# Moving half of an output projection in among attention units, in a one-core streaming-encoder layer

## The chip, the cores and the metric

The kernel runs on one core of a Trainium2 chip. The time is device microseconds of that core for one launch; the profile is one execution of its own, recorded by the hardware profiler. TensorE does the matmuls and transposes, ScalarE, VectorE and GpSimd the rest, and nearly all transfers are issued from SyncE's queue (SP).

## What is computed

One layer for 1024 prompt tokens and 32 sample tokens (1056 rows of 1024). Cut to what matters here:

```python
proj = x @ w_in
o_a = latent attention, 8 heads of 64            # "A", 512 columns of mix
o_b = rms(differential attention, 4 heads of 128)  # "B", 512 columns of mix
mix = concatenate([o_a, o_b], -1)
h = LN1(ALPHA * x + mix @ w_o)
h = LN2(ALPHA * h + ConvGLU(h))
y = h + sigmoid(h @ w_ple_gate + b) * (p @ w_ple_proj)
```

All of it is in 32-bit precision. A matmul of the projections runs as three matmuls on a split of each operand into a high and a low part (`three`, lines 144 to 146); for the sample rows as two (`sample_rows`, lines 152 and 153). Splitting (`split`) is a ScalarE copy of the high part (line 85) and a VectorE subtraction of it (line 82).

## The kernel before, in words

The program is traced in Python and then planned: each engine gets a static list in an order that a planner makes from the order in the text and from its own costs, and tiles take slots of small pools: 22 `pair`s (`HP`, tag h) for most operands, 4 `slab`s, 2 `stg`, 2 `srow`, and in PSUM 4 banks `pm` and 2 double banks `pd`. `paced` and `held` put an instruction in the plan not ahead of the last marked one; they add no wait on the chip.

- Attention is 32 units of `UnitB` (4 heads, 8 row blocks from the last to the first) and then 64 of `UnitA` (8 heads). `front` makes a block's scores (lines 554 and 555 for B, `three` into `pd` for A), the softmax's maximum on VectorE (line 524) and the exponential on ScalarE. `back` comes two or three units later; it transposes the probabilities (lines 575 and 804), copies them out of PSUM (line 576; a `split` in A) and multiplies with the values (lines 579 and 813). `hook(n, ...)` puts other work ahead of unit n: preparation of keys and queries (`prep_a`, `unpark`, with copies in SBUF through SP at lines 731 and 756), and the sample rows' latent attention at 84 to 95.
- The results are `mixB` (B, features by tokens) and `mixA` (A).
- The output projection comes after attention, for the sample tile 8 and then tiles 7 to 0: once with `w_o` columns 0 to 255 for all nine, once with 256 to 511, each with all eight blocks of 128 features, B's first (the two passes of the loop over `i`), and then with columns 512 to 1023 inside `h_rows`. `mix_in` splits a tile's four feature pairs; `residual` (line 1026) adds ALPHA times x, which `x_back` has loaded.
- `h_rows` goes on with the first norm (`unit`), `h_turn` transposes the normed row and applies gain and bias (line 1087 on TensorE, line 1090 on VectorE and 1092 on ScalarE in turns), and `h_pair` and `h_sample` make the sums of blocks (`combos`) with which the up-projection does seven block products instead of eight. `UpWeights.part` makes the weights' sums; the first pair's seven parts run in the second pass of the projection.
- The up-projection (lines 1205 to 1207), from 731 us on, the down-projection and the gate follow; the change does not touch them.

Of the kernel before, what the change touches and what calls it, by code (L numbers as in the profile page):

```python
# [16 lines left out]
DEC = 32  # L17
# [20 lines left out]
def layer(ctx: ExitStack, tc: tile.TileContext, a, o):  # L38
# [497 lines left out]
    class UnitB:  # L536
# [26 lines left out]

        def back(self):
            h, i, p2 = self.h, self.i, self.p
            ss = UnitB.group[h, i // 4]
            if i % 4 == 3:
                UnitB.po = pm((128, 4, 128))
            po = UnitB.po
            pT = slab((128, 8, 128))  # L570
            for k0 in range(0, i + 1, 4):
                kn = min(4, i + 1 - k0)
                pt = pm((128, 4, 128))
                for j in range(kn):
                    PE.transpose(pt[:, j], p2[:, 0, (k0 + j) * 128 : (k0 + j + 1) * 128], ident)
                ACT.copy(pT[:, k0 : k0 + kn], pt[:, :kn])
            ii = i % 4
            for k in range(i + 1):
                PE.matmul(po[:, ii], pT[:, k], dv[k // 4][:, k % 4, h * 128 : (h + 1) * 128], start=(k == 0), stop=(k == i))  # L579
            ACT.activation(pT[:, 0], po[:, ii], AF.Square, accum_out=ss[:, 4 + ii : 5 + ii])  # L580
            if ii:
                return

            DVE.scalar_tensor_tensor(ss[:, 8:12], ss[:, 0:4], EPS, ss[:, 0:4], ALU.mult, ALU.mult)
            DVE.scalar_tensor_tensor(ss[:, 8:12], ss[:, 4:8], 1.0 / 128.0, ss[:, 8:12], ALU.mult, ALU.add)
            POOL.tensor_tensor(ss[:, 12:16], ss[:, 8:12], neghalf[:, 0:1].to_broadcast([128, 4]), ALU.pow)
            ob = srow() if h == 3 else small(512, tag="sam", bufs=1)
            for q in range(4):
                DVE.scalar_tensor_tensor(ob[:, q * 128 : (q + 1) * 128], po[:, q], ss[:, 12 + q : 13 + q], g8, ALU.mult, ALU.mult)
            hook(UnitB.step + 3, lambda: self.finish(ob))  # L590
# [176 lines left out]
    class UnitA:  # L767
# [20 lines left out]

        def back(self):
            h, i, p = self.h, self.i, self.p  # L790
            vt = L["vt"][h // 4]
            j, ib = divmod(i, 2)
            kt = 2 * (j + 1)
            if ib:
                UnitA.pts = [pair((128, 2, 4, 256)) for _ in range((kt + 3) // 4)]
            pts = UnitA.pts
            if i in (7, 3):
                UnitA.po = pm()
            po = UnitA.po
            for k0 in range(0, i + 1, 4):  # L800
                kn = min(4, i + 1 - k0)
                pt = pm((128, 4, 128))
                for jj in range(kn):
                    PE.transpose(pt[:, jj], p[:, (k0 + jj) * 128 : (k0 + jj + 1) * 128], ident)  # L804
                d = pts[k0 // 4]
                UnitA.turned = split(d[:, 0, :kn, 128 * ib : 128 * ib + 128], d[:, 1, :kn, 128 * ib : 128 * ib + 128], pt[:, :kn])
            if ib:
                POOL.memset(f(pts[-1][:, :, (kt - 1) % 4, 0:128]), 0.0)
                return
            c = 256 * (j % 2)  # L810
            for k in range(kt):
                for hl in range(2):
                    PE.matmul(po[:, c : c + 256], vt[k // 4][:, k % 4, h % 4], pts[k // 4][:, hl, k % 4],  # L813
                              start=(k == 0 and hl == 0), stop=(k == kt - 1 and hl == 1))
            if j % 2 == 0:
                e = h % 2
                own, oth = slice(64 * e, 64 * e + 64), slice(64 - 64 * e, 128 - 64 * e)
                d = hd(L["mixA"], h // 2)[own, 256 * j : 256 * j + 512]
                ACT.copy(d, po[oth])
                DVE.tensor_tensor(d, po[own], d, ALU.add)  # L820
# [101 lines left out]
                ACT.copy(L["mixA"][g][64 * e : 64 * e + 64, :, S0:T], v[64 * e : 64 * e + 64, 2 * g : 2 * g + 2, e])  # L922

    w_o = a["w_o"].rearrange("(k p) c -> p k c", p=128)
    wb = []

    def wo_block(c, N):
        per = 1024 // N
        return [wload([(0, 1024, w_o[:, (4 + i * per) % 8 : (4 + i * per) % 8 + per, c : c + N])], 1024) for i in range(8 // per)]


    units = [UnitB(h, i) for h in range(4) for i in range(7, -1, -1)]
# [32 lines left out]
    for n, s in enumerate((sa_load, sa_query, lambda: sa_keys(0), lambda: sa_keys(1), sa_rotary, lambda: sa_scores(0),  # L965
                           lambda: sa_scores(1), lambda: sa_turn(0), lambda: sa_turn(1), lambda: sa_values(0), lambda: sa_values(1), sa_end)):
        hook(84 + n, s)
    hook(94, lambda: gate.__setitem__(0, UnitA.last), lambda: wb.append(wo_block(0, 256)))

    waiting = []  # L970
    for n in range(len(units)):
        UnitB.step = n
        for s in hooks.setdefault(n, []):
            s()
        units[n].front()
        waiting.append(units[n])
        while len(waiting) > (2 if n < 8 or n >= 32 else 3):
            waiting.pop(0).back()
    for n, u in enumerate(waiting):
        for s in hooks.get(len(units) + n, ()):  # L980
            s()
        u.back()
    mixA = L["mixA"]
    gate[0], mark[0] = UnitA.last, UnitA.turned


    acc = [pair((128, 2, 1024), F32) for _ in range(4)]
    acc_s = cpool.tile([DEC, 1024], F32, name="acc_s", tag="x4")
    order = (8, 7, 6, 5, 4, 3, 2, 1, 0)

# [2 lines left out]


    mixp = {}
    msam = small(512, F32R, tag="sam", bufs=1).rearrange("p (k h c) -> p k h c", k=8, h=2)

    def mix_in(t):

        c0, n = TOK[t]  # L1000
        d = mixp[t] = pair((128, 8, 2, 128)) if t < 8 else msam
        for i in range(4):
            src = (mixB if i < 2 else mixA)[i % 2][:, :, c0 : c0 + n]
            split(d[:, 2 * i : 2 * i + 2, 0, :n], d[:, 2 * i : 2 * i + 2, 1, :n], src, pace=t < 7)

    mix_in(8)

    def proj_rows(t, wk, N):

        n = TOK[t][1]  # L1010
        ps = pm()
        d = mixp[t]
        if t < 8:
            three(ps[:, :N], [(d[:, k, 0], d[:, k, 1], *wk(k)) for k in range(8)])
            return ps[:, :N], None
        sample_rows(ps, lambda k: d[:, k].rearrange("p h c -> p (h c)"), wk, 8, N)
        return ps[:DEC, :N], ps[DEC : 2 * DEC, :N]

    def wo_at(ws, N):
        per = 1024 // N  # L1020
        return lambda k: tuple(ws[k // per][:, hl, (k % per) * N : (k % per + 1) * N] for hl in (0, 1))

    def residual(t, c, N, ps, ps2):
        n = TOK[t][1]
        d = arow(t)[:n, c : c + N]
        mark[0] = DVE.scalar_tensor_tensor(d, d, ALPHA, ps, ALU.mult, ALU.add)
        if ps2 is not None:
            lo = small(512, tag="srow", bufs=2)
            ACT.copy(lo[:n, :N], ps2)
            DVE.tensor_tensor(d, d, lo[:n, :N], ALU.add)  # L1030

    def unit(r, n):

# [11 lines left out]
        (eng or POOL).tensor_tensor(r, r, g[:n, :D], ALU.mult)  # L1045
        (eng or POOL).tensor_tensor(r, r, b[:n, :D], ALU.add)

    def x_back(t):
        load(arow(t)[: TOK[t][1]], a["x_p"][t * 128 : (t + 1) * 128, :] if t < 8 else a["x_s"])

    for t in order[:3]:
        x_back(t)
    for t in order[1:3]:
        mix_in(t)

# [24 lines left out]
    def h_turn(t, d):  # L1082

        n = TOK[t][1]
        ps = pd((128, 8, 128))
        for j in range(8):
            PE.transpose(ps[:, j, :n], arow(t)[:n, j * 128 : (j + 1) * 128], ident[:n, :n])
        for j in range(8):
            if j % 2:
                DVE.tensor_scalar(d[:, j], ps[:, j, :n], lnT[:, j : j + 1], lnT[:, 8 + j : 9 + j], ALU.mult, ALU.add)  # L1090
            else:
                ACT.activation(d[:, j], ps[:, j, :n], AF.Identity, bias=lnT[:, 8 + j : 9 + j], scale=lnT[:, j : j + 1])
# [153 lines left out]
    zd = [DR.tile([128, len(fs), T], F32, name=nm("zd")) for fs in GROUPS]  # L1246


    for i in range(2):
        for m, t in enumerate(order):  # L1250
            if i == 0:
                if m == 1:
                    wb.append(wo_block(256, 256))
                if 2 < m + 2 < 9:
                    x_back(order[m + 2])
                    if m:
                        mix_in(order[m + 2])
            elif m == 0:
                wb.append(wo_block(512, 512))
                wts = UpWeights(up_load(0))  # L1260
            if i == 1 and m < NP:
                wts.part(m)
            ps, ps2 = proj_rows(t, wo_at(wb[i], 256), 256)
            residual(t, 256 * i, 256, ps, ps2)


    hrow = [DR.tile([128, 1024], F32, name=nm("hrow")) for _ in range(8)]

    def h_rows(t):
        ps, ps2 = proj_rows(t, wo_at(wb[2], 512), 512)  # L1270
        residual(t, 512, 512, ps, ps2)
        unit(arow(t)[: TOK[t][1]], TOK[t][1])
        if t < 8:
            SP.dma_start(hrow[t], arow(t))


    for t in order[:4]:
        h_rows(t)
    hs = small(512, tag="sam", bufs=1)
    V["hs"], V["hs2"] = hs[:, :256].rearrange("p (k c) -> p k c", k=8), hs[:, 256:512]  # L1280
    h_turn(8, V["hs"])
# [330 lines left out]
```

## Time and profile before

| | |
|---|---|
| median of 3 runs | 1582.12 us (1577.77 to 1582.86) |
| the profiled execution's own time | 1580.15 us |
| its span in the profile | 1578.1 us, mean granted clock 0.986 |
| TensorE busy | 1506.7 us (95%) |
| VectorE, ScalarE, GpSimd busy | 970.7, 716.5, 336.8 us |
| differential units | about 252 to 352 us |
| latent units and their preparation | about 352 to 594 us |
| projection, first norm, block sums | about 594 to 731 us |

All stretches are microseconds from the start of the span. A matmul's busy time holds its way through the array, and consecutive matmuls overlap, so a stretch in which TensorE is shown busy need not be full. Rows of waits name the waiting engine and line, then what released it. "clock" is the granted share of TensorE's full speed.

### The profile page before, as it was taken

Reading aid. Unit: us, or ns where it says so; the run is one execution under the profiler, and the core shown is the slowest. Engines: PE = TensorE matmul, PEld = TensorE weight load, DVE = VectorE, ACT = ScalarE, POOL = GpSimd, SP = SyncE. Lnnn points to the kernel's source line nnn. Section 1 sums busy time; section 2 is a strip of 40 time slices with the busy share of each in tenths; the row PEclk is TensorE's granted clock in tenths of the full one; section 3 lists DMA queues with packets and bytes.
Section 4 is the critical chain, followed back from the end, with each engine's and each line's share of the span. In section 5 each row is a group of like instructions: output and inputs, shape, how many; then the busy total and the mean of one; then the engine's idle time right before and its main releaser. Section 6 shows DMA issues by size and latency. Waiting matters only on the chain.

```text
span 1578.1 us, 25308 instructions
## 1 busy us (share of the span) xinstructions
PE 1506.7 (95%) x9787; PEld 1363.0 (86%) x9787; DVE 970.7 (62%) x1944; ACT 716.5 (45%) x1754; POOL 336.8 (21%) x394
## 2 busy tenths in 40 slices
PE   7999998888989999989999999999989999999998
PEld 7999987777878889878999999999977787876887
DVE  4113336885767757598577777777778524279332
ACT  4223337776777765056455555555543312022111
POOL 0002134632454320010011111111110000049311
PEclk9999999989999999999999999999999999999999
DMA  7113251221110116122222222222265423231111
GB/s 218 38 46 89 81 159 46 43 63 28 25 49 15 51 54 208 41 87 62 80 82 82 82 82 82 82 74 68 91 194 171 146 59 115 80 99 42 41 44 44
DMA packets 125868, 127.89 MB, mean 81 GB/s; under 512 B 14701, under 2 KB 105461, under 8 KB 125493
## 3 DMA queue, kind: packets, MB, share of 16 engines
q1 hardware_dynamic: 125749, 126.28, 26.3%
q8 instruction: 77, 1.26, 0.3%
q14 instruction: 42, 0.34, 0.1%
HBM read 93.83 MB, written 26.07 MB: 76 GB/s over the span
## 4 chain that ended last, share of the span: by engine, by line
PE 81%; DVE 10%; ACT 5%; DMA 2%; issue 2%; POOL 0%; SPq 0%; DVEq 0%; ACTq 0%
PE pm L144 13%; PE pm L146 13%; PE pm L145 13%; PE pd L1207 5%; PE pd L1206 5%; PE pd L1205 5%; PE pm L1205 4%; PE pm L1207 4%; PE pm L1206 4%; DVE h L82 3%; PE pm L813 2%; ACT h L85 2%; PE pm L579 1%; PE pm L804 1%; DVE h L562 1%
## 5 line engine op out<-in xcount | busy, mean ns | idle before, releaser
L144 PE MATMUL pm<-h,h 128*128 128x512 f32 (+4 forms) x1076 | 367.6, 342 | 6.3 <-DVE h L82 3.6
L146 PE MATMUL pm<-h,h 128*128 128x512 f32 (+4 forms) x1076 | 364.4, 339 | 3.6 <-DVE h L82 3.6
L145 PE MATMUL pm<-h,h 128*128 128x512 f32 (+4 forms) x1076 | 363.8, 338 | 0.0
L144 PEld LDWEIGHTS pm<-h,h 128*128 128x128 f32 x1076 | 204.7, 190 | 28.4 <-issue 3.2
L146 PEld LDWEIGHTS pm<-h,h 128*128 128x128 f32 x1076 | 203.5, 189 | 23.7 <-DVE h L82 4.2
L145 PEld LDWEIGHTS pm<-h,h 128*128 128x128 f32 x1076 | 203.8, 189 | 19.5 <-issue 0.5
L85 ACT CAST h<-t 128x1024 fp32r<-128x1024 f32 (+6 forms) x91 | 81.9, 912 | 216.5 <-PE pm L146 102.0
L82 DVE TENSOR_TENSOR h<-t,h 128x1024 fp32r<-128x1024 f32 (+6 forms) x81 | 89.5, 1114 | 96.5 <-ACT h L85 96.3
L82 DVE TENSOR_TENSOR h<-pm,h 128x256 fp32r<-128x256 f32 (+7 forms) x221 | 101.6, 485 | 55.8 <-ACT h L85 53.9
L1218 DVE SCALAR_TENSOR_TENSOR h<-h,cp,h 128x1058 f32<-128x1058 f32 x88 | 115.8, 1316 | 25.4 <-ACT h L1226 24.7
L85 ACT CAST h<-pm 128x256 fp32r<-128x256 f32 (+7 forms) x221 | 88.5, 426 | 53.7 <-PE pm L804 22.1
L1192 ACT COPY h<-pd 128x256 f32<-128x256 f32 (+1 forms) x258 | 56.1, 270 | 115.9 <-PE pd L1207 115.8
L1205 PE MATMUL pm<-h,s 128*128 128x264 f32 x360 | 102.7, 288 | 1.2 <-ACT h L1192 0.9
L1206 PE MATMUL pm<-h,s 128*128 128x264 f32 x360 | 102.0, 286 | 0.4 <-DVE h L82 0.4
L82 DVE TENSOR_TENSOR h<-h,h 128x512 fp32r<-128x512 f32 (+4 forms) x166 | 100.7, 638 | 2.2 <-ACT h L85 2.1
L1207 PE MATMUL pm<-h,s 128*128 128x264 f32 x360 | 99.9, 286 | 0.0
L1205 PE MATMUL pd<-h,s 128*128 128x264 f32 x344 | 97.9, 285 | 0.4 <-DVE h L1090 0.4
L1206 PE MATMUL pd<-h,s 128*128 128x264 f32 x344 | 97.8, 284 | 0.5 <-DVE h L82 0.5
L1207 PE MATMUL pd<-h,s 128*128 128x264 f32 x344 | 98.1, 285 | 0.0
L1367 DVE TENSOR_TENSOR h<-pm,h 128x512 f32<-128x512 f32 x48 | 32.8, 684 | 76.4 <-PE pm L146 76.3
L178 POOL TENSOR_TENSOR sm<-sm,neghalf 128x1 f32<-128x1 f32 (+1 forms) x37 | 23.9, 645 | 253.6 <-DVE sm L177 239.1
L82 DVE TENSOR_TENSOR s<-h,s 128x512 fp32r<-128x512 f32 (+1 forms) x96 | 60.4, 639 | 28.5 <-ACT s L85 28.2
(326 smaller groups left out, 3734.2 us busy)
## 6 DMA issues: line engine op xcount, KB each, us to landing
h<-in_w_up SPq DMA_DIRECT2D x44, 512.0 KB, 4.7
zd<-h SPq DMA_DIRECT2D x22, 529.0 KB, 4.4
t<-zd SPq DMA_DIRECT2D x24, 384.0 KB, 3.6
t<-in_w_down SPq DMA_DIRECT2D x16, 512.0 KB, 3.2
h<-in_x_p SPq DMA_DIRECT2D x15, 512.0 KB, 7.2
t<-in_w_in SPq DMA_DIRECT2D x14, 512.0 KB, 3.8
h<-h SPq DMA_DIRECT2D x8, 512.0 KB, 4.9
t<-in_w_o SPq DMA_DIRECT2D x8, 512.0 KB, 3.4
```

Of the source, the lines that this page charges most:

```text
L82: return eng.tensor_tensor(out, x, y, ALU.subtract)
L85: c = ACT.copy(hi, src)
L144: PE.matmul(ps, sh, mh, start=(i == 0), stop=False)
L145: PE.matmul(ps, sh, ml, start=False, stop=False)
L146: PE.matmul(ps, sl, mh, start=False, stop=(i == last))
L813: PE.matmul(po[:, c : c + 256], vt[k // 4][:, k % 4, h % 4], pts[k // 4][:, hl, k % 4], start=(k == 0 and hl == 0), stop=(k == kt - 1 and ...
L1192: ACT.copy(x, y)
L1205: PE.matmul(ps[:, :BW], w[:, 0, k], c[:, k, 0], start=first and k == 0, stop=False, skip_group_check=True)
L1206: PE.matmul(ps[:, :BW], w[:, 0, k], c[:, k, 1], start=False, stop=False, skip_group_check=True)
L1207: PE.matmul(ps[:, :BW], w[:, 1, k], c[:, k, 0], start=False, stop=k == 3, skip_group_check=True)
L1218: DVE.scalar_tensor_tensor(z[:, j], U[:, j, i : i + T], cp[:, i, m + j * NF : m + j * NF + 1], z[:, j], ALU.mult, ALU.add)
L1367: DVE.tensor_tensor(d, ps[:n], d, ALU.add)
```

## The change

The projection is split by feature half. The B half (blocks 4 to 7 of `w_o`) is done in 36 pieces, four blocks of 256 columns times nine token tiles, hooked ahead of units 38 to 46, 47 to 55, 66 to 74 and 75 to 83, one to a unit. A block loads and splits its weights (`share_w`); a mix tile pair is split once, in the first block, written to DRAM (`hb`) and loaded again in the other three (`share_in`, one unit ahead). A piece (`share`) loads 256 columns of x into an `srow`, does four blocks of three matmuls (for the sample tile two) into a `pm` bank, adds ALPHA times x on VectorE and stores the sum to DRAM (`xw`). The A half is one pass after attention, in `h_rows`: two times 512 columns with four blocks, on rows loaded from `xw`, with the norm right behind. The values of a unit, in A and B, are done one unit after its transposes (`values`). In `h_turn` ScalarE takes columns 0 to 3 and VectorE 4 to 7. The seven parts of the first up-weights run two behind each of the first four `h_rows`.

```diff
@@ class UnitB, UnitA
         def back(self):
...
+        def values(self):
+            h, i, pT = self.h, self.i, self.pT
+            ss = UnitB.group[h, i // 4]
+            if i % 4 == 3:
+                UnitB.po = pm((128, 4, 128))
...
+        def values(self):
+            h, i = self.h, self.i
+            vt = L["vt"][h // 4]
+            j, ib = divmod(i, 2)
+            if ib:
                 return
+            kt = 2 * (j + 1)
+            if i in (6, 2):
+                UnitA.po = pm()
+            po, pts = UnitA.po, self.pts
...
+    def wo_rows(k):
+        wA.append(wload([(0, 1024, w_o[:, k])], 1024))
...
+    def share_w(b):
+        st = stg()
+        paced(SP.dma_start(st[:, :1024].rearrange("p (k c) -> p k c", k=4), w_o[:, 4:8, 256 * b : 256 * b + 256]))
+        F["w"] = w = pair()
+        split(w[:, 0, :1024], w[:, 1, :1024], st[:, :1024], pace=True)
+
+    def share_in(b, q):
+        d = F["d", q] = pair((128, 2, 4, 2, 128) if q < 4 else (128, 4, 2, DEC))
+        if b:
+            paced(SP.dma_start(f(d), hb[q]))
+            return
+        for e in range(2 if q < 4 else 1):
+            c0, n = TOK[2 * q + e]
+            v = d[:, e] if q < 4 else d
+            for i in range(2):
+                src = mixB[i][:, :, c0 : c0 + n]
+                split(v[:, 2 * i : 2 * i + 2, 0], v[:, 2 * i : 2 * i + 2, 1], src, pace=True)
+        SP.dma_start(hb[q], f(d))
+
+    def share(b, t):
+        n = TOK[t][1]
+        cs = slice(256 * b, 256 * b + 256)
+        x = srow()[:n, :256]
+        paced(SP.dma_start(x, a["x_p"][t * 128 : (t + 1) * 128, cs] if t < 8 else a["x_s"][:, cs]))
+        ps = pm()
+        w, d = F["w"], F["d", t // 2]
+        wk = lambda k: (w[:, 0, 256 * k : 256 * k + 256], w[:, 1, 256 * k : 256 * k + 256])
+        if t < 8:
+            three(ps[:, :256], [(d[:, t % 2, k, 0], d[:, t % 2, k, 1], *wk(k)) for k in range(4)])
+        else:
+            sample_rows(ps, lambda k: d[:, k].rearrange("p h c -> p (h c)"), wk, 4, 256)
+        DVE.scalar_tensor_tensor(x, x, ALPHA, ps[:n, :256], ALU.mult, ALU.add)
...
+        SP.dma_start(xw[t][:, cs], x)
...
+    for b in range(4):
+        base = (38, 47, 66, 75)[b]
+        hook(base - 1, lambda b=b: share_w(b))
+        for m, t in enumerate((4, 5, 6, 7, 0, 1, 2, 3, 8)):
+            if t % 2 == 0:
+                hook(base + m - 1, lambda b=b, t=t: share_in(b, t // 2))
+            hook(base + m, lambda b=b, t=t: share(b, t))
-    hook(94, lambda: gate.__setitem__(0, UnitA.last), lambda: wb.append(wo_block(0, 256)))
+    hook(94, lambda: gate.__setitem__(0, UnitA.last), lambda: [wo_rows(k) for k in range(2)])
...
         units[n].front()
         waiting.append(units[n])
+        if turned:
+            turned.pop(0).values()
         while len(waiting) > (2 if n < 8 or n >= 32 else 3):
-            waiting.pop(0).back()
+            turned.append(waiting.pop(0))
+            turned[-1].back()
+        while len(turned) > 1:
+            turned.pop(0).values()
...
+        for i in range(2):
+            split(d[:, 2 * i : 2 * i + 2, 0], d[:, 2 * i : 2 * i + 2, 1], mixA[i][:, :, c0 : c0 + n])
+
+    def x_back(t):
+        if t % 2:
+            acc[t // 2] = pair((128, 2, 1024), F32)
+        load(arow(t)[: TOK[t][1]], xw[t])
...
+        r = arow(t)[:n, c : c + 512]
+        mark[0] = DVE.tensor_tensor(r, ps[:n], r, ALU.add)
...
         for j in range(8):
-            if j % 2:
+            if j >= 4:
                 DVE.tensor_scalar(d[:, j], ps[:, j, :n], lnT[:, j : j + 1], lnT[:, 8 + j : 9 + j], ALU.mult, ALU.add)
...
-    for i in range(2):
-        for m, t in enumerate(order):
...
-            ps, ps2 = proj_rows(t, wo_at(wb[i], 256), 256)
-            residual(t, 256 * i, 256, ps, ps2)
...
     def h_rows(t):
-        ps, ps2 = proj_rows(t, wo_at(wb[2], 512), 512)
-        residual(t, 512, 512, ps, ps2)
+        for c in (0, 512):
+            proj_rows(t, c)
+        m = order.index(t) + 3
+        if m < 9:
+            mix_in(order[m])
+            x_back(order[m])
         unit(arow(t)[: TOK[t][1]], TOK[t][1])
...
-    for t in order[:4]:
+    wts = UpWeights(up_load(0))
+    for m, t in enumerate(order[:4]):
         h_rows(t)
+        for i in range(2 * m, min(2 * m + 2, NP)):
+            wts.part(i)
```

## Rows read from the trace of the kernel before

**Rows 1.** The page, first part: TensorE's matmuls and weight loads, busy time and instructions, then the other engines.

```profile
PE 1506.7 (95%) x9787; PEld 1363.0 (86%) x9787; DVE 970.7 (62%) x1944; ACT 716.5 (45%) x1754; POOL 336.8 (21%) x394
```

**Rows 2.** Busy times by stretch: its length, busy time and instructions of each engine, the granted clock, the share of the DMA engines and GB/s.

```profile
252.00:352.00 100.00, 84.26 (x534) 71.17 (x533) 85.43 (x237) 78.97 (x219) 48.14 (x37) 0.93 0.21 47
352.00:399.00 47.00, 40.75 (x267) 36.40 (x267) 29.25 (x90) 33.75 (x110) 12.11 (x14) 0.93 0.13 31
399.00:455.00 56.00, 52.11 (x342) 45.96 (x341) 39.80 (x112) 39.46 (x97) 28.50 (x40) 1.00 0.15 37
455.00:490.00 35.00, 29.68 (x181) 26.31 (x180) 25.59 (x64) 26.22 (x70) 19.07 (x23) 0.95 0.14 32
490.00:533.00 43.00, 40.32 (x269) 36.12 (x268) 33.36 (x87) 32.06 (x76) 20.58 (x29) 1.00 0.06 14
533.00:594.00 61.00, 56.14 (x376) 48.60 (x375) 37.73 (x95) 42.80 (x108) 15.03 (x25) 1.00 0.25 77
594.00:646.00 52.00, 52.00 (x429) 50.90 (x428) 33.67 (x70) 19.75 (x44) 0.00 (x0) 1.00 0.42 142
...
646.00:731.00 85.00, 77.67 (x421) 66.49 (x420) 71.50 (x169) 38.40 (x104) 7.07 (x13) 0.94 0.22 75
```

**Rows 3.** The timeline of TensorE in the projection: start, duration, line, operands, count. Two neighbours of 256 columns, two of 512, and a run of eight transposes.

```profile
609.98 0.28 PE L145 MATMUL pm<-h,h 128*128 128x256 f32 x1
610.10 0.29 PE L146 MATMUL pm<-h,h 128*128 128x256 f32 x1
...
655.79 0.40 PE L145 MATMUL pm<-h,h 128*128 128x512 f32 x1
656.03 0.39 PE L146 MATMUL pm<-h,h 128*128 128x512 f32 x1
...
670.35 1.03 PE L1087 MATMUL pd<-ident,h 128*128 128x128 f32 x8
```

**Rows 4.** The groups of TensorE's matmuls in the stretch 399 to 455, shapes kept apart: count, busy time and mean duration, idle time before them. Each group of line 144 has two more like it at lines 145 and 146 (of 256 columns into `pm`, 9 each).

```profile
L813 PE MATMUL pm<-h,h 128*128 128x256 f32 x92 | 16.2, 297 | 3.0 <-ACT h L85 2.6 <-DVE h L82 0.3
L804 PE MATMUL pm<-ident,s 128*128 128x128 f32 x75 | 11.5, 273 | 0.1
L144 PE MATMUL pd<-h,h 96*128 96x512 f32 x15 | 6.6, 439 | 0.3 <-DVE sm L524 0.3
...
L144 PE MATMUL pm<-h,h 128*128 128x256 f32 x10 | 2.9, 292 | 0.0
...
L144 PE MATMUL pd<-h,h 96*128 96x256 f32 x9 | 2.7, 305 | 0.5 <-DVE sm L524 0.4
...
L804 PE MATMUL pm<-ident,t 128*128 128x128 f32 x12 | 2.3, 274 | 0.0
L144 PE MATMUL pm<-h,h 128*128 128x352 f32 x6 | 1.9, 324 | 0.0
...
L144 PE MATMUL pd<-h,h 96*128 96x384 f32 x5 | 1.9, 380 | 0.0
...
L144 PE MATMUL pm<-h,h 128*128 128x512 f32 x4 | 1.6, 395 | 0.0
...
L144 PE MATMUL pm<-h,h 128*128 128x354 f32 x4 | 1.3, 323 | 0.0
```

**Rows 5.** The groups of TensorE's matmuls in the stretch 594 to 646, of which line 144 stands for its two siblings and line 152 for 153.

```profile
L144 PE MATMUL pm<-h,h 128*128 128x256 f32 x128 | 36.0, 281 | 0.0
...
L152 PE MATMUL pm<-h,sm 128*64 128x256 f32 x16 | 3.8, 279 | 0.0
```

**Rows 6.** Groups of VectorE in the stretch 594 to 731: remainders of mix tiles (256 wide), of weights (1024 wide), and residuals.

```profile
L82 DVE TENSOR_TENSOR h<-h,h 128x256 fp32r<-128x256 f32 x28 | 10.0, 418 | 0.0
L82 DVE TENSOR_TENSOR h<-t,h 128x1024 fp32r<-128x1024 f32 x6 | 7.3, 1221 | 4.8 <-ACT h L85 4.8
L1026 DVE SCALAR_TENSOR_TENSOR h<-h,pm 128x256 f32<-128x256 f32 x16 | 6.6, 414 | 10.8 <-PE pm L146 10.8
L1026 DVE SCALAR_TENSOR_TENSOR h<-h,pm 128x512 f32<-128x512 f32 x8 | 5.5, 684 | 6.8 <-PE pm L146 6.8
```

**Rows 7.** TensorE's waits in 252 to 360: total us, times, longest.

```profile
PE pm L579 <- ACT s L576: 4.2, 6, 1.4
...
PE pm L575 <- ACT s L576: 2.1, 1, 2.1
```

**Rows 8.** TensorE's waits in 360 to 595.

```profile
PE pm L813 <- ACT h L85: 7.4, 8, 1.3
PE pm L144 <- DVE h L82: 3.6, 2, 2.5
PE pd L144 <- DVE sm L524: 2.9, 6, 0.7
```

**Rows 9.** Busy times in the stretch 676 to 712, columns as in rows 2.

```profile
676.00:712.00 36.00, 31.25 (x169) 26.98 (x169) 35.12 (x84) 22.02 (x61) 3.79 (x5) 0.91 0.30 97
```

**Rows 10.** ScalarE's waits in 660 to 731.

```profile
ACT h L1092 <- DVE h L1090: 10.8, 12, 3.0
```

**Rows 11.** Transfers by source: count, KB each, median us from issue to landing.

```profile
h<-in_w_up SPq DMA_DIRECT2D x44, 512.0 KB, 4.7
...
t<-in_p_p SPq DMA_DIRECT2D x8, 128.0 KB, 2.9
```

**Rows 12.** The SP queue's own waits in 252 to 600.

```profile
SPq L756 <- PE pd L146: 57.9, 3, 25.4
```

More of the change, by code (lines that the diff above doesn't have):

```diff
@@ L565, in back @@
             h, i, p2 = self.h, self.i, self.p
[L566 to L570, printed above, removed]
+            pT = self.pT = slab((128, 8, 128))
             for k0 in range(0, i + 1, 4):
@@ L576, in back @@
                 ACT.copy(pT[:, k0 : k0 + kn], pt[:, :kn])
+        def values(self):
[3 more added lines that the diff above has]
+                UnitB.po = pm((128, 4, 128))
+            po = UnitB.po
             ii = i % 4
@@ L790, in back @@
             h, i, p = self.h, self.i, self.p
-            vt = L["vt"][h // 4]
             j, ib = divmod(i, 2)
@@ L795, in back @@
                 UnitA.pts = [pair((128, 2, 4, 256)) for _ in range((kt + 3) // 4)]
[L796 to L799, printed above, removed]
+            pts = self.pts = UnitA.pts
             for k0 in range(0, i + 1, 4):
@@ L924, in layer @@
     w_o = a["w_o"].rearrange("(k p) c -> p k c", p=128)
[L925 to L929, printed above, removed]
+    wA = []
+    def wo_rows(k):
+        wA.append(wload([(0, 1024, w_o[:, k])], 1024))
+    hb = [DR.tile([128, 2, 4, 2, 128], F32, name=nm("hb")) for _ in range(4)] + [DR.tile([128, 4, 2, DEC], F32, name=nm("hb"))]
+    xw = [DR.tile([128, 1024], F32, name=nm("xw")) for _ in range(8)] + [DR.tile([DEC, 1024], F32, name=nm("xw"))]
+    F = {}
+    def share_w(b):
[28 more added lines that the diff above has]
+        DVE.scalar_tensor_tensor(x, x, ALPHA, ps[:n, :256], ALU.mult, ALU.add)
+        if t == 8:
+            lo = srow()[:n, :256]
+            ACT.copy(lo, ps[n : 2 * n, :256])
+            DVE.tensor_tensor(x, x, lo, ALU.add)
+        SP.dma_start(xw[t][:, cs], x)
     units = [UnitB(h, i) for h in range(4) for i in range(7, -1, -1)]
@@ L967, in layer @@
         hook(84 + n, s)
-    hook(94, lambda: gate.__setitem__(0, UnitA.last), lambda: wb.append(wo_block(0, 256)))
-    waiting = []
+    for b in range(4):
[6 more added lines that the diff above has]
+    hook(94, lambda: gate.__setitem__(0, UnitA.last), lambda: [wo_rows(k) for k in range(2)])
+    waiting, turned = [], []
     for n in range(len(units)):
@@ L982, in layer @@
         u.back()
+        for v in turned:
+            v.values()
+        turned = [u]
+    turned[0].values()
     mixA = L["mixA"]
     gate[0], mark[0] = UnitA.last, UnitA.turned
-    acc = [pair((128, 2, 1024), F32) for _ in range(4)]
+    acc = {}
     acc_s = cpool.tile([DEC, 1024], F32, name="acc_s", tag="x4")
@@ L995, in layer, with proj_rows @@
     mixp = {}
-    msam = small(512, F32R, tag="sam", bufs=1).rearrange("p (k h c) -> p k h c", k=8, h=2)
     def mix_in(t):
         c0, n = TOK[t]
[L1001 to L1008, printed above, removed]
+        if t == 8:
+            mixp[8] = small(512, F32R, tag="sam", bufs=1)[:, :256].rearrange("p (k h c) -> p k h c", k=4, h=2)
+        elif t % 2:
+            V["mp"] = pair((128, 2, 4, 2, 128))
+        d = mixp[t] = mixp[8] if t == 8 else V["mp"][:, t % 2]
+        for i in range(2):
[4 more added lines that the diff above has]
+        load(arow(t)[: TOK[t][1]], xw[t])
+    def proj_rows(t, c):
         n = TOK[t][1]
@@ L1012, in proj_rows @@
         d = mixp[t]
+        wk = lambda k: (wA[k][:, 0, c : c + 512], wA[k][:, 1, c : c + 512])
         if t < 8:
[L1014 to L1030, printed above, removed]
+            three(ps, [(d[:, k, 0], d[:, k, 1], *wk(k)) for k in range(4)])
+        else:
+            sample_rows(ps, lambda k: d[:, k].rearrange("p h c -> p (h c)"), wk, 4, 512)
+        r = arow(t)[:n, c : c + 512]
+        mark[0] = DVE.tensor_tensor(r, ps[:n], r, ALU.add)
+        if t == 8:
+            lo = srow()
+            ACT.copy(lo[:n], ps[n : 2 * n])
+            DVE.tensor_tensor(r, r, lo[:n], ALU.add)
     def unit(r, n):
@@ L1046, in norm @@
         (eng or POOL).tensor_tensor(r, r, b[:n, :D], ALU.add)
-    def x_back(t):
-        load(arow(t)[: TOK[t][1]], a["x_p"][t * 128 : (t + 1) * 128, :] if t < 8 else a["x_s"])
+    for k in range(2, 4):
+        wo_rows(k)
     for t in order[:3]:
+        mix_in(t)
         x_back(t)
-    for t in order[1:3]:
-        mix_in(t)
     BW = 264
@@ L1246, in layer @@
     zd = [DR.tile([128, len(fs), T], F32, name=nm("zd")) for fs in GROUPS]
-    for i in range(2):
-        for m, t in enumerate(order):
[L1251 to L1262, printed above, removed]
-            ps, ps2 = proj_rows(t, wo_at(wb[i], 256), 256)
-            residual(t, 256 * i, 256, ps, ps2)
     hrow = [DR.tile([128, 1024], F32, name=nm("hrow")) for _ in range(8)]
     def h_rows(t):
-        ps, ps2 = proj_rows(t, wo_at(wb[2], 512), 512)
-        residual(t, 512, 512, ps, ps2)
+        for c in (0, 512):
[4 more added lines that the diff above has]
+            x_back(order[m])
         unit(arow(t)[: TOK[t][1]], TOK[t][1])
```

## Prediction

> **What bounds the kernel now.** I read the page's first part, then the busy times by stretch, then the starts of single matmuls, then the waits. TensorE is busy 1506.7 of 1578.1 us [rows 1]. The stretches [rows 2] show three regimes around the change: the differential units (252 to 352), the latent units with their preparation (352 to 594), and the output projection with the first norm (594 to 731), of which 594 to 646 is nothing but 256-column projection matmuls (PE busy 52.00 of 52) and 646 to 731 holds the 512-column third of the projection, the norms and the block sums for the up-projection. The granted clock is 1.00 or close to it in most of them.
>
> Busy time hides slack, since matmuls overlap. Their starts show what one costs in a dense run: 256 columns 0.12 us (I use 0.118), 512 columns 0.235 us (I use 0.233), a transpose 0.11 us (eight in 1.03 less the tail) [rows 3]. Applied to the stretch 399 to 455, the latent units 38 to 55: 256 columns 92 + 3 x (10 + 9) = 149, so 17.6 us; 87 transposes, 9.6; 512 columns 3 x (15 + 4) = 57, 13.3; 352 and 354 columns 30 at 0.162, 4.9; 384 columns 15 at 0.175, 2.6 [rows 4]. That is 48 of 56 us, 86%; the slack is 8 us where the busy row shows 3.9. The stretch 490 to 533, units 66 to 83, issues matmuls at the same rate (269 in 43 us against 342 in 56 [rows 2]), so it has 6 more. **14 us of slack, then, in all 36 unit slots that will get a piece.**
>
> **The change, part by part.** *The pieces.* 32 pieces of 12 matmuls of 256 columns, 32 x 12 x 0.118 = 45.3 us, and 4 sample pieces of 8, 3.8 us: 49.1 us of TensorE work enter the two stretches. As many leave 594 to 646: three times 128 matmuls, and 32 for the sample rows, all of 256 columns [rows 5]. The columns are the same before and after, so no TensorE work is saved; the only gain there can be is slack that gets filled. The two stretches need 48 + 37 + 49 = 134 us of 99 + x. Bounds: all 14 us filled, x = 35; the whole at today's 86%, x = 57. A piece depends on nothing of the unit it stands in, so it can run while a transposed tile is evacuated; but each engine runs its list in order and a piece takes one of the four `pm` banks until its residual is done. I take 95%, x = **+42**.
>
> *What the pieces bring beside matmuls.* On VectorE 36 residuals at 0.41, four weight remainders at 1.22, 16 remainders of the mix tiles at 0.42: 27 us with the durations of [rows 6]. The two stretches have VectorE at 39.8 + 33.4 of 99 us; 100 of 141 afterwards. ScalarE gets some 11 us on 71.5. I cost both at nothing, hidden by TensorE; without that cover it would be the 27 us. On the SP queue, four weight loads, 36 loads of 128 KB, 36 stores, 5 stores and 15 reloads of whole mix tiles (1 MB each but for the sample's). Nothing on TensorE waits for the first two kinds; TensorE does wait for a reload.
>
> *Values one unit later.* TensorE stands idle for the evacuated transposes ahead of the values: 4.2 and 2.1 us in the differential units [rows 7], 7.4 us in the latent ones [rows 8]. With another unit's scores in between, the copy is done. Bounds: 0, if the next wait (a score bank that waits for the softmax, 2.9 us [rows 8]) takes the place, and 13.7. The differential stretch is also VectorE's, 85.4 of 100 us, so I take **-5**.
>
> *The projection after attention.* The stretch 594 to 646 (52 us) goes. What is left of the pass per token tile is two 512-column halves of 12 matmuls, 24, as many as the third block of today has, so TensorE's work in 646 to 731 stays what it is. VectorE's does not. Today it has 33.67 us of work before 646 and 71.50 behind [rows 2]. Away go 16 mix remainders (6.7 us), four weight remainders (4.9) and about 1 us of residuals, as 16 of 256 and 8 of 512 columns become 16 of 512 [rows 6]: 12.6 us. So 92.6 us have to fit where TensorE needs 24 x 0.233 x 8 = 45 for the tiles, 4 for the sample, 8 for 72 transposes and 10 for the first up-products, 67 us in all. **VectorE becomes the bound of this stage**; today it already is from 676 to 712, busy 35.12 of 36 [rows 9]. Some 5 us of it (the last weights, the first three mix tiles) can run under the last units. Bounds: 85 us as today, if the idle 13.5 us of VectorE take it all, and 92.6 / 0.95 = 98 with nothing run early. I take 93, nearer to the sum: -52 + 8 = **-44**. What is late next is the last pair of block sums, for which the up-projection waits as it does now.
>
> *The first norm's turn* gives ScalarE columns 0 to 3 and VectorE 4 to 7, where they alternate now. ScalarE waits 10.8 us in 12 places for VectorE's neighbouring piece [rows 10]. The number of operations on each stays, and where VectorE is the bound a ScalarE wait costs nothing: it is inside the 93 (bounds 0 and -3).
>
> *Weights, x, up-weights.* Two rows of `w_o` are still loaded under the last units and two behind, `x` comes back already scaled and summed; the up-weights' seven parts move under the first four norms and are counted in VectorE's 92.6.
>
> **Sum:** +42 - 5 - 44 = -7 us. Against the profiled execution's own 1580.15 that is 1573; the median of the runs shown, 1582.12, lies 2 above that execution, so **1575 us**. All bounds at their good ends give 35 - 14 - 55 = -34, at their bad ends 57 + 0 - 39 = +18. A measurement of this kernel tells 0.3%, 4.7 us, from no change, so 1575 is just on the faster side.
>
> **Rivals.** *(1) Slower, by late mix tiles.* A reload is issued one unit ahead of its piece. A unit of these stretches takes 99 / 36 = 2.75 us, with its piece about 4. A 512 KB load lands after a median 4.7 us, one of 128 KB after 2.9 [rows 11], so 1 MB lands later than one unit by some us unless it is issued further ahead in the queue. A piece whose tile is late holds all of TensorE, scores included. The SP queue is also in order, and entries in it wait long today: 57.9 us in three waits of the rotary rows' copies for the scores that read the old ones [rows 12]; loads of `x` stood behind one would delay a residual and hold its bank. 15 reloads at 1.5 us each are 23 us: 1575 + 23 = 1598. It decides from 7 / 15 = 0.5 us each. Against it: TensorE's waits of 360 to 595 hold next to none for a transfer, all larger ones are for ScalarE and VectorE [rows 8], so the planned order leaves room for landings.
>
> *(2) The slack is one of buffers.* TensorE's waits there are not all for data: 3.6 and 2.9 us are for a bank that VectorE has yet to read [rows 8]. If that is what the 14 us consist of, a piece only adds to the demand for banks, fills nothing, and x is 49 with nothing from the later values: +49 - 44 = +5, 1587. The Trainium skill (Perfetto Trace Analysis, Optimization Strategy) speaks for this case: gaps that repeat on the engine that should be full can mean that no buffer is free for the next tile. The trace agrees in part; the largest wait, 7.4 us, is for data.
>
> *(3) More is filled.* The pieces take all but 2 of the 14 us (x = 37), the later values 10, and VectorE's stage is 89 us: 37 - 10 - 48 = -21, 1561. For it speaks that TensorE runs with no gap wherever independent work is at hand (594 to 646).
>
> **How the numbers follow.** The sum as worked out 0.45, (3) 0.15, (2) 0.18, (1) 0.22. The likeliest case alone spans 1564 to 1586 (x from 37 to 49, the last stage from 88 to 98). For 8 in 10 the range goes to (3) and beyond it to 1554, and to (1) at 1598. Faster by over 0.3%, under 1577.4: most of the first case (0.35), all of (3): 0.50. Within: 0.10 of the first and 0.10 of (2): 0.20. Slower, over 1586.9: 0.08 of (2) and (1): 0.30.
>
> **What would show it.** In the profile after: TensorE's stretch of the pieces about 42 us longer than the 99 of now, at 95% of dense spacing; the last values at about 631 instead of 594; no stretch of pure 256-column matmuls; from there to the unbroken up-projection about 93 us with VectorE over 95% busy and TensorE at some 70%; ScalarE's waits for VectorE in the turn gone. Wrong would make it: TensorE waiting for a reload of a mix tile or for the piece's weights for more than 0.5 us each; the stage after attention at 85 or below (then VectorE was not its bound); VectorE or the banks, rather than TensorE, setting the pace of units 38 to 83; or a granted clock well under 1 in the last stage, where TensorE is now idle for a third of the time: today it falls to 0.91 where VectorE sets the pace [rows 9].

## The result, and the profile after

The changed kernel takes 1601.1 us (median of 4 runs, 1600.59 to 1602.58) against 1582.07 before: ratio 1.0127, 95% interval 1.0108 to 1.0147, some 20 us slower. 1575 was forecast, 1598 the upper end of the range.

The profiled execution has a span of 1598.8 us. Its busy times by stretch, columns as in [rows 2]. The first stretch ends where the first pieces run; the pieces' residuals run from 408 to 492 and from 524 to 599, so most of them stand in 399 to 480 and in 513 to 613; at 656 the last values are done. The last row goes on to where the up-projection runs without a break:

```profile
352.00:399.00 47.00, 42.40 (x295) 37.79 (x293) 30.73 (x99) 35.36 (x115) 16.93 (x21) 1.00 0.16 40
...
399.00:480.00 81.00, 72.91 (x520) 66.91 (x521) 53.57 (x140) 45.35 (x111) 25.46 (x34) 1.00 0.56 190
480.00:513.00 33.00, 27.11 (x161) 23.66 (x160) 20.75 (x56) 23.44 (x64) 17.53 (x18) 0.95 0.18 43
513.00:613.00 100.00, 90.34 (x630) 82.77 (x629) 59.24 (x149) 54.20 (x122) 28.39 (x45) 0.97 0.52 166
613.00:656.00 43.00, 37.77 (x240) 32.75 (x238) 24.53 (x56) 27.64 (x65) 9.31 (x14) 1.00 0.22 78
656.00:748.00 92.00, 75.72 (x392) 62.71 (x393) 85.89 (x201) 43.48 (x118) 7.39 (x11) 0.91 0.35 119
...
656.00:754.00 98.00, 81.68 (x439) 68.46 (x440) 91.89 (x212) 46.98 (x130) 10.60 (x13) 0.91 0.33 112
```

TensorE is no fuller than it was before: from 399 to attention's end it is busy 228.1 of 257 us (the rows from 399 to 656 above), and [rows 2] have 178.2 of 195 from 399 to 594. The DMA share in the stretches with pieces is 0.56 and 0.52, where it was 0.15 and 0.06. The last values, 593.9 us before, are at 655.3:

```profile
654.98 0.62 PE L822 MATMUL pm<-h,h 128*128 128x256 f32 x3 [0.90 <-DVE h L82]
660.97 0.83 PE L1192 MATMUL pm<-ident,t 44*128 44x44 f32 x6 [5.37 <-DMA t<-in_conv_w]
```

So attention ends 61.4 us later. From there to the 400th matmul of the up-projection it takes 128.9 us instead of 167.3, 38.4 less. (61.4 - 38.4 = 23; the span grew by 20.7. The 2.3 us between them lie behind that matmul, in code that the change leaves alone: that part takes between 812.6 and 817.7 us in the profiles of this case. So a stretch read from one profile is sure to some 3 us, not better.)

Who waits in the stretch of the pieces: the SP queue, VectorE, then TensorE, in 380 to 640 (380 to 660 for TensorE). Line 970 loads a piece's x, line 978 is its residual, 983 its store, 981 the second copy of a sample piece.

```profile
SPq L970 <- DMA xw<-sm: 42.1, 25, 4.6
SPq L983 <- DVE sm L978: 35.3, 14, 9.4
```

```profile
DVE sm L978 <- DMA sm<-in_x_p: 14.6, 10, 2.5
...
DVE sm L978 <- PE pm L146: 9.7, 6, 3.8
...
DVE sm L978 <- DMA sm<-in_x_s: 3.7, 2, 2.3
```

```profile
PE pd L144 <- DVE sm L524: 5.9, 11, 1.1
PE pm L822 <- ACT h L85: 5.3, 4, 3.0
PE pm L144 <- DVE sm L978: 3.4, 4, 1.6
PE pm L144 <- DMA h<-hb: 2.6, 2, 1.4
PE pm L144 <- ACT sm L981: 2.1, 1, 2.1
PE pm L803 <- ACT sm L981: 1.8, 1, 1.8
...
PE pm L152 <- DVE sm L978: 0.6, 1, 0.6
```

The load of x waits in 25 places until the *store* of two pieces earlier has landed, since the two share a buffer; the residual then waits for x; and TensorE waits for the bank that the residual holds. The reload itself (`h<-hb`), which the prediction's slower rival was about, is waited for 2.6 us in all.

### The profile page after: what moved, and what is told of

The parts are those of the page before. It is cut to its first block, busy times and chain, and to the rows that moved or that the text cites. A ratio compares the mean times of both kernels' runs of the same rounds, so it can differ in the third digit from the quotient of the medians.

```text
span 1598.8 us, 25611 instructions
## 1 busy us (share of the span) xinstructions
PE 1509.0 (94%) x9787; PEld 1363.6 (85%) x9787; DVE 980.2 (61%) x1974; ACT 718.0 (45%) x1757; POOL 343.8 (22%) x394
## 4 chain that ended last, share of the span: by engine, by line
PE 74%; DVE 10%; DMA 6%; ACT 5%; issue 2%; POOL 1%; SPq 0%; DVEq 0%; ACTq 0%; POOLq 0%
PE pm L144 12%; PE pm L146 12%; PE pm L145 12%; PE pd L1276 5%; PE pd L1274 5%; PE pd L1275 5%; PE pm L1274 4%; PE pm L1276 4%; PE pm L1275 4%; DVE h L82 4%; ACT h L85 2%; DMA xw<-sm 1%; DMA sm<-in_x_p 1%; PE pm L822 1%; PE pm L152 1%
## 5 line engine op out<-in xcount | busy, mean ns | idle before, releaser
L144 PE MATMUL pm<-h,h 128*128 128x512 f32 (+4 forms) x1076 | 369.6, 344 | 12.5 <-DVE sm L978 3.4
L82 DVE TENSOR_TENSOR h<-h,h 128x512 fp32r<-128x512 f32 (+5 forms) x168 | 102.7, 643 | 2.1 <-ACT h L85 2.1
L119 POOL TENSOR_SCALAR s<-s,sm 128x1024 f32<-128x1024 f32 (+8 forms) x56 | 45.6, 814 | 149.4 <-DVE sm L789 114.0
```

What stands on the lines that cost most here:

```text
L82: return eng.tensor_tensor(out, x, y, ALU.subtract)
L119: return eng.tensor_scalar(out, x, s, 0.0, ALU.mult, ALU.add)
L144: PE.matmul(ps, sh, mh, start=(i == 0), stop=False)
```

## The experiments

Times are medians of one job; the kernel before stood at 1579.7 to 1580.7 in these jobs. "Attention end" is the last values' matmul in the profile. The changed kernel's 1601.1 comes from a job in which the kernel before stood at 1582.07, so differences to it are 1 to 2 us smaller when both are taken as ratios to the kernel before.

**What do the pieces cost?** All 36 left out; the B half is missing from the output and x comes from the input.

```diff
-    for b in range(4):
-        base = (38, 47, 66, 75)[b]
...
-    load(arow(t)[: TOK[t][1]], xw[t])
+    load(arow(t)[: TOK[t][1]], a["x_p"][t * 128 : (t + 1) * 128, :] if t < 8 else a["x_s"])
```

> The changed kernel without its 36 pieces: the B half of the projection is left out, and x comes back from the input instead of the stored sums. The pieces' price is the changed kernel's 1601 less this. If they cost what the prediction gave (42): 1559. If they fill nothing and cost no more than their matmuls (49): 1552. If they also bring waits of their own (62 to 66, as the unit starts of the two profiles have it): 1535 to 1539. In all three cases the stage after attention should stay at some 93 us.

1537.6 us; attention ends at 592.8, and from there to the 400th up-projection matmul it takes 129.0 us, as in the changed kernel. The pieces cost 63.5 us (62 by the ratios), 62.5 of them ahead of attention's end: all of their 49 us of matmuls and 13 more.

**Are the transfers the excess?** First the pieces without x and without their store (their result is lost), then without the reloads (blocks 1 to 3 multiply one tile pair of block 0), then without both.

```diff
-        paced(SP.dma_start(x, a["x_p"][t * 128 : (t + 1) * 128, cs] if t < 8 else a["x_s"][:, cs]))
...
-        DVE.scalar_tensor_tensor(x, x, ALPHA, ps[:n, :256], ALU.mult, ALU.add)
+        DVE.tensor_scalar(x, ps[:n, :256], ALPHA, 0.0, ALU.mult, ALU.add)
...
-        SP.dma_start(xw[t][:, cs], x)
```

> The changed kernel whose pieces neither load their columns of x nor store the sum: VectorE only takes the bank out into the small buffer, by one operation of the same size; the pieces' result is left out of the output. What stays: matmuls, weights, mix tiles and their reloads. Theory 'small-buffer ring' (two buffers, each held from the load's issue to the store's landing, set the pace of the pieces and hold PSUM banks): 10 to 15 us faster than the changed kernel, 1586 to 1591. Theory 'no slack to fill': 1601 within 3, as TensorE has the same matmuls.

```diff
         if b:
-            paced(SP.dma_start(f(d), hb[q]))
+            F["d", q] = F["d", 2] if q < 4 else F["d", 4]
             return
```

> The changed kernel without the 15 reloads of mix tiles: blocks 1 to 3 use one tile pair of block 0 (and the sample's) for all token tiles, so their products are those of other tokens. Theory 'late mix tiles' (the prediction's first rival, 1.5 us for each of 15): 1579. By the profile after, where TensorE's waits for the reload come to 2.6 us: 1598 to 1601. If the reloads slow the other transfers in the queue, in between.

> The changed kernel with both left out: the pieces' x and sums (as e6) and the reloads (as e7); matmuls, weights and bank evacuations stay, the output lacks the pieces. e6 was 15.8 and e7 11 faster than the changed kernel's 1601. If the two costs are separate: 1574, a price of 37 for the pieces over the 1537.6 without them, which would fill 12 of the 14 us of slack that the prediction counted. If they are one cost seen twice (the SP queue): 1582 to 1586, and no slack is filled.

1585.3, 1590.0 and 1581.3 us; attention ends at 639.1, 643.8 and 635.2. Each alone gives back 16.2 or 11.5 us of the stretch, both 20.1: they overlap. Without them (the four weight loads and the five stores of mix tiles are still there) the pieces cost 635.2 - 592.8 = **42.4 us, the price forecast (42)**; by the medians it is 43.6. The other 20 come with these transfers and with what the edits take away beside them, among it the `pair` slots of the reloaded tiles.

**Two buffers, or too many transfers?** The changed kernel with one edit: x in a large tile of eight slots per block. As many loads, stores and reloads as before.

```diff
+        F["x"] = pair((128, 8, 256), F32)
...
-        x = srow()[:n, :256]
+        x = F["x"][:, t] if t < 8 else srow()[:n, :256]
```

> The changed kernel with one thing mended: the pieces' x sits in one large tile of eight slots per block instead of two small buffers. Mix tiles are stored and reloaded as in the changed kernel, and so is the number of transfers. Theory 'the two buffers are what the prediction missed, the reloads cost by standing in their cycle': about what the kernel with neither transfer took, 1581 to 1585. Theory 'the reloads cost 11 by themselves': 1590 or more. If the large tile is one too many beside the reloaded ones: 1595 or more.

1584.4 us, attention end at 640.0: 15 us faster by the ratios (16.7 by the medians), by the buffers and the plan that they allow, with the reloads in place. VectorE no longer waits for x, except 0.7 us once, for the sample rows; its residual (line 979 here) waits for TensorE, and TensorE's waits for the residual's bank have shrunk from 7.9 us in all to under 1:

```profile
DVE h L979 <- PE pm L146: 12.7, 13, 3.2
```

```profile
PE pd L144 <- DVE sm L524: 7.6, 10, 2.4
PE pm L822 <- ACT h L85: 2.4, 3, 1.1
PE pm L144 <- DVE h L82: 1.5, 2, 1.3
...
PE pm L144 <- DMA h<-hb: 0.9, 1, 0.9
```

The same question asked from kernels without reloads, where the mix tiles are split again in each block (and with the mended order of the next experiment): with two buffers, with eight slots and two transfers per block each way, and with eight slots and a load and a store per piece.

> A kernel with the right output: e4's order, and the mix tiles of every block are split again from the attention's result on ScalarE and VectorE, instead of stored and reloaded. Takes 48 more splits of 256 columns (20 us of VectorE, 19 of ScalarE), and the two tiles of B stay until the last block. Theory 'the reloads cost 11 by transfers': with e4's 8, 1582. Theory 'ScalarE and VectorE or the buffers are short': 1593 or more.

> e9 with one large tile per block for x: eight slots of 256 columns, loaded by two transfers per block and stored by two, in the place of two small buffers that turn round once per piece. Theory 'small-buffer ring': some 15 us faster than e9, around 1567 to 1572, and faster than both kernels. If the ring was no cost by itself but the SP queue was, about as e9; if one more large buffer is too many, slower than e9.

> The kernel with one large x tile per block (e10), but each piece loads and stores its own slot, as in the changed kernel: as many transfers in the SP queue as there, eight buffers instead of two. It tells the two readings of the small-buffer cost apart. Theory 'two buffers': as e10's 1584, within 3. Theory 'so many transfers in one queue': near e9's 1594.

1594.0, 1583.7 and 1581.4 us. For the prompt tiles, 32 single loads and stores are as good as eight bundled transfers each way (the sample tile has four single ones in both): the number of transfers doesn't matter here, the number of buffers does, 10 to 13 us (9 to 11 by the ratios). Splitting again in place of reloading is worth little once the buffers are there (1581.4 against 1584.4).

**The wait behind attention.** TensorE's 5.4 us for the convolution constants:

```diff
-    for k in range(2, 4):
-        wo_rows(k)
-    for t in order[:3]:
-        mix_in(t)
-        x_back(t)
...
     ucol = cpool.tile([128, 4, NM], F32, name="ucol", tag="y2")
+    for k in range(2, 4):
+        wo_rows(k)
+    for t in order[:3]:
+        mix_in(t)
+        x_back(t)
```

> The changed kernel with one order mended: the convolution constants (loads, transposes) stand in the text ahead of the last two weight rows and the first three tiles of the A half, not behind them. In the profile after, TensorE stands 5.4 us before those transposes for their load and then runs eight matmuls at half the granted clock. Theory 'that wait was a cost of its own': 7 to 9 us faster, 1592 to 1594. Theory 'the next load is as late' (x sums, weight rows): 1599 to 1601.

1599.5 us, 1.6 less than the changed kernel (0.8 by the ratios): a miss. That wait is gone, but attention's end to the 400th matmul of the up-projection is 128.1 us where it was 128.9. Something else sets the stage's length. (Attention ends at 658.9 in this profile, 3.6 later than in the changed kernel's, though the edit lies behind it; part of that is the granted clock, which in 350 to 355 is 0.69 here and 1.00 there.)

**What bounds the stage after attention?** The first up-weights' sums and remainders on GpSimd, in the kernel with bundled slots:

```diff
-    wts = UpWeights(up_load(0))
+    wts = UpWeights(up_load(0), POOL)
...
-            split(w[:, 0], w[:, 1], src)
+            split(w[:, 0], w[:, 1], src, self.eng)
```

> e10 with the first up-weights' four sums and seven remainders on GpSimd instead of VectorE. Theory 'VectorE is the bound of the stage after attention' (busy 90 of 96 us in e10's profile): 6.6 us less on it, 1577 to 1580. Theory 'the order of waits bounds it': no change, 1584 within 3; slower if GpSimd is late with a part that TensorE waits for.

1577.5 us, 6.2 less; the stage takes 124.3 us against 128.5. (The rest of the profiles' difference lies ahead of attention's end, which the edit doesn't touch.) That fits VectorE as the bound; the kernel with bundled slots shows it busy for 90 of 96 us behind attention:

```profile
639.00:735.00 96.00, 79.27 (x416) 67.00 (x415) 90.29 (x210) 46.48 (x128) 12.20 (x13) 0.91 0.36 126
```

Carried further, with the differences of three of the four block sums on GpSimd too (on the kernel with single transfers):

> The pieces with eight slots and mix tiles split again (e11, 1581), with the first up-weights' sums and remainders on GpSimd (6 us in e13) and, of the block sums, the four differences of the first three pairs on GpSimd too. VectorE is the bound of the stage after attention: 7.2 us less on it by 12 operations of 0.6. Theory holds on: 1569 to 1573. If GpSimd's longer operations become what is waited for: 1575 or more.

1585.0 us, a miss, 3.6 more than with nothing on GpSimd: the stage is back at 129.5. GpSimd is busy 42.93 of 96 us and VectorE still 90.07, though some 16 us of work have left it (an estimate: 23 operations of 0.69). What is left on it runs slower. Two of its groups, first in the kernel with single transfers (636 to 732), then here (641 to 737):

```profile
L82 DVE TENSOR_TENSOR h<-h,h 128x512 fp32r<-128x512 f32 x30 | 19.7, 690 | 0.0
...
L82 DVE TENSOR_TENSOR h<-h,h 128x256 fp32r<-128x256 f32 x16 | 5.8, 409 | 0.0
```

```profile
L82 DVE TENSOR_TENSOR h<-h,h 128x512 fp32r<-128x512 f32 x26 | 23.7, 929 | 0.0
...
L82 DVE TENSOR_TENSOR h<-h,h 128x256 fp32r<-128x256 f32 x16 | 9.9, 659 | 0.0
```

Of the 26, the 14 that overlap no GpSimd operation (those of line 178 not counted) take 0.68 us on average, the 12 that do take 1.22, up to 1.78. The residuals on line 1099, which read a PSUM bank, take 0.67 in both kernels. These two groups alone lose 10 us. In the run before this one the second group already takes 656 ns. So most of what GpSimd takes over is paid for again on VectorE. Beside that, ScalarE waits 15.6 us (in 641 to 770) for what GpSimd makes, and TensorE 7.3 at one place for the block products' evacuation on ScalarE; what each of these is worth was not separated.

**Pieces behind their unit.** The pieces' text moved behind the unit's scores, transposes and values (bundled slots). The sample piece of blocks 0 and 2 meets the next block's weights in it and multiplies with these.

> e10 with each piece's text behind its unit's scores, transposes and values instead of ahead of them, so that in the plan the piece only takes what the unit leaves; weights and mix tiles are loaded as early as in e10. Theory 'the pieces fill little because they go first': 5 to 10 us faster than e10's 1584. Theory 'the slack is one of buffers and order within the units': as e10, within 3; or slower, if a later piece holds its bank or tile longer.

1588.0 us, 4.3 slower than with the pieces first. That the pieces fill little because they go first isn't borne out.

**The two other parts alone.** On the kernel before: the values one unit later, as in the change; then only

```diff
-            if j % 2:
+            if j >= 4:
                 DVE.tensor_scalar(d[:, j], ps[:, j, :n], lnT[:, j : j + 1], lnT[:, 8 + j : 9 + j], ALU.mult, ALU.add)
```

and then both.

> The kernel before with one part of the change alone: the values of a unit one unit after its transposes, in A and B; nothing else is changed. By the prediction's term (-5): 1577. By the profile after, where the differential stretch 252 to 352 has the same dense matmul time in the same length (PE busy 83.94 there against 84.26): no change, 1582 within 3. If the later values hold buffers that the next units want, slower, 1586 or more.

> The kernel before with one part of the change alone: ScalarE takes columns 0 to 3 of the first norm's turn and VectorE 4 to 7. By the prediction (0, bounds 0 and -3): 1580 within 3 beside the 1580 of the kernel before in these runs.

> The kernel before with two parts of the change and nothing else: the values one unit later, and ScalarE and VectorE on halves of the first norm's turn. Alone they took 4.6 and 4.5 us off the kernel before. If they add up: 1571, faster than both kernels. If both gained by the same stall after attention, 1575.

1575.35 (ratio 0.9963, interval 0.9950 to 0.9976), 1576.16 (0.9967, 0.9954 to 0.9979) and **1571.27 us (0.9950, 0.9936 to 0.9963)**, faster than both kernels. With the values alone attention ends 2.3 us earlier in the profile, with both 5.0; the turn stands behind attention, so the 2.7 between them show how far one profile can be trusted. TensorE's waits with the values alone, 252 to 360, beside [rows 7]:

```profile
PE pm L571 <- DVE h L562: 4.8, 5, 2.1
PE pm L571 <- ACT s L572: 2.1, 1, 2.1
PE pm L616 <- ACT s L572: 2.0, 2, 1.5
PE pd L554 <- DVE sm L524: 1.4, 4, 0.5
PE pm L582 <- ACT s L583: 1.3, 3, 0.7
PE pm L582 <- ACT s L572: 1.1, 3, 0.5
```

The wait ahead of the values fell from 4.2 to 1.1 us. The transposes wait for the probabilities (line 562) 4.8 us instead of 2.5, and other transposes (line 616) 2.0 us for ScalarE; before, it was

```profile
PE pm L575 <- DVE h L562: 2.5, 1, 2.5
```

In the latent units (360 to 592) the values wait 5.7 us where [rows 8] have 7.4, and the scores 4.1 instead of 2.9 for their bank.

## Why the prediction was wrong, point by point

**The step that failed is a term at nothing:** of the pieces' transfers the prediction says "Nothing on TensorE waits for the first two kinds" (the weight loads and the loads of x) and gives the stores no price at all, so +42 holds matmuls alone. As built the term is +20. TensorE waits for no x itself; it waits for buffers. The prediction named the `pm` bank that a piece holds until its residual, and named loads of x that might stand behind another wait, but did not work out the cycle: an `srow` is taken by the load, the residual and the store, and free when the store has landed. In the changed profile a load lands after a median 2.8 us (1.8 to 7.6) and a store after 2.3 (1.5 to 4.9). With the residual's 0.42 and two issues of 0.33, that is an estimate of 6.2 us per piece and 3.1 with two buffers, if nothing else waits. With eight slots a piece comes about every 4 us (residuals from 409 to 484 and from 517 to 584), so 3.1 alone would still fit. But the sample piece takes both buffers, 1 MB transfers stand in between, and `rotary` takes both in units 52 to 56; how much each of these adds was not measured. One sign of being wrong that the prediction named, banks that hold up units 38 to 83, is there in TensorE's waits. The result is 15 us of stretch (655.3 against 640.0), shown by changing the buffers and nothing else in the text. TensorE's visible waits for lines 978 and 981 come to 7.9 us; how the rest divides between waits of other engines and a plan that puts the pieces further apart was not separated. The Trainium skill (DMA: Bandwidth & Descriptors, Latency and other measured facts) puts the fixed cost of a transfer at about 2 us, most of it the round trip of the receipt from the memory that is written. The shortest store here, 1.5 us, is near it. A buffer here stands through two landings, one of its load and one of its store.

**The pieces' own price was right.** +42 forecast, 42.4 measured without x, sums and reloads (43.6 by the medians): 6 or 7 of the 14 us of slack are filled. As built it was 62.5, past even the bad bound of 57, which held no wait of the pieces' own. (The 27 us that the prediction adds up for VectorE come to 26.4, and four of its 36 loads and stores are of the sample's 32 KB; nothing turns on it.)

**The slower rival was right in direction, and its size (1598) came near by luck.** It was to be late mix tiles, 1.5 us for each of 15. Reloads are waited for 2.6 us; taking them out gains 11.5, but only 4 once the x ring is out too (639.1 to 635.2). So most of their cost shows only beside the two buffers. Without reloads x lands after a median 2.2 us instead of 2.8, and VectorE waits for it 12.5 us instead of 18.3, while the loads wait for the stores as long as before (42.4 us). That fits transfers that stand in each other's way in one queue; the slots that the reloaded tiles take were not separated from it. The other rival, slack of buffers, has a share: TensorE's largest remaining waits with eight slots are for a score bank that VectorE has yet to read (7.6 us).

**Values one unit later** (-5): attention ends 2.3 us earlier, the whole kernel takes 4.6 less. As bounded, other waits took most of the place: the probabilities in the differential units, the score bank in the latent ones. What is gained shows in 352 to 399, where the granted clock is 1.00 with the later values alone, with both parts and in the changed kernel, and 0.93 in [rows 2] and with the turn alone. Why some 2 us more are gained behind attention is open; the granted clock there is 0.99 in this profile (591 to 728) and 0.96 in the one of the kernel before (594 to 731), which may be chance.

**The turn** (0, bounds 0 and -3): 4.5 us on the kernel before, interval 3.3 to 7.3, so under-sized. The argument was that a ScalarE wait costs nothing where VectorE is the bound; the alternation cost more than that. In the changed profile ScalarE's waits for VectorE's neighbour (10.8 us in [rows 10]) are gone from the turn, as the prediction said. Its larger waits for prompt tiles are now

```profile
ACT h L85 <- DVE h L82: 14.4, 5, 4.2
ACT h L1161 <- PE pd L1155: 7.9, 3, 3.1
ACT h L85 <- DVE h L1159: 3.9, 2, 2.6
```

that is, for VectorE's remainders (5.5 us before, in 594 to 731; 14.7 with the turn alone), for TensorE's transposes and twice for VectorE's half. So ScalarE's idle time has moved, not gone, and by which wait the turn gains 4.5 us is open; some 2 of them show in the profile's stage.

**The stage after attention** (-44, bounds -52 and -39): -38.4, just outside the bad bound. VectorE became the engine that is busy nearly throughout, as argued, and its work is what was forecast: 91.89 us in 656 to 754, 92.6 in the prediction. What was sized too small is the idle time beside it: the sum took 93 us for the stage, close to none, and VectorE is at 94%, with 6 us idle. TensorE waits there 5.7 us for the block products (line 1274). The granted clock is 0.91, as the prediction feared.

**The sum** as measured: +42.4 for the pieces, +20.1 for their transfers, -38.4 for the stage, and -1.1 for the rest ahead of attention's end (593.9 to 592.8, where -5 was forecast): +23 up to the 400th matmul of the up-projection, against -7. 20 of these 30 us are the transfers that were priced at nothing.

## What to carry to other kernels

Work that is moved into another stage as filler brings its buffers' cycle with it: from the load's issue to the store's landing, divided by the number of buffers. Count it before calling a transfer hidden: here an estimated 3.1 us in a slot of about 4 left no room for what else used these buffers and their queue. Slack that is spread as waits inside dependent units fills only in part, here 7 of 14 us, with 49 us of work that needed nothing of the units it stood in. And when half of a stage is taken away, look which engine's work stays behind: here VectorE's did, so 49 us of matmuls left a stage that became 38 us shorter. Giving that engine's work to another helps only if it doesn't slow what stays.

## What the runs showed of the hardware that was not expected

32 loads and 32 stores of 128 KB through one queue cost no more than eight bundled transfers each way (1581.4 against 1583.7 us), once there were buffers to land in. Two engines that take the columns of a double PSUM bank by halves gained 4.5 us over taking them in turns, with the same number of operations on each; whether the bank or the order of the plan makes the difference was not separated. And subtractions on VectorE with both inputs in SBUF took up to 1.78 us instead of 0.68 while GpSimd was working (12 of 26 overlapped it, 1.22 on average); the residuals, with one input in PSUM, kept their 0.67.
